# A two-layer decoder trunk: the second layer's modulation sums moved from VectorE to ScalarE and GpSimd, with three smaller moves beside them

## The chip, the cores and the metric

The kernel runs on one core of a Trainium2 chip. A core has five engines that work side by side: TensorE (PE in the profile; its weight loads are the row PEld), VectorE (DVE), ScalarE (ACT), GpSimd (POOL) and SyncE (SP), which here does nothing but issue transfers between the device's main memory and the on-chip memory. Each engine runs its own instructions in the order in which they were put there, and waits on semaphores for the others. The metric is device time in microseconds (us) of one launch. Results are compared by the median of several runs.

## The reference, cut to what matters

Everything is float32, for one sequence of 1024 positions of width 1024, in two layers:

```python
c_act = silu(c)                                    # one vector of 1024
for l in range(2):
    mod = c_act @ ada_w[l] + ada_b[l]              # 1024 x 6144: six vectors of 1024
    shift_m, scale_m, gate_m, shift_f, scale_f, gate_f = split(mod, 6)
    h = rms_norm(x, g_pre_mix[l]) * (1 + scale_m) + shift_m
    q, k, v, u = split(h @ w_in[l] + b_in[l])      # 512, 128, 128, 512
    attn = sliding-window attention with sinks and partial rotary (q, k, v)
    pool = causal means over 2, 4, 8, 16 positions of u, mapped and scaled
    x = x + gate_m * rms_norm(concat(attn, pool) @ w_out[l], g_post_mix[l])
    h = rms_norm(x, g_pre_ffn[l]) * (1 + scale_f) + shift_f
    f = (silu(h @ w_gate[l]) * (h @ w_up[l])) @ w_down[l]      # inner width 2816
    x = x + gate_f * rms_norm(f, g_post_ffn[l])
```

The vector `mod` depends on `c` and on the weights alone, so it can be made at any time before it is used. Its weights are 24 MB for each layer.

## The kernel before, in words

**Products.** A float32 operand is split into a rounded part `hi` (one ScalarE copy, line 213) and the rest `lo` (one VectorE subtraction, line 214; both stand in the helper `split`). A product is then three matmuls, hi by hi, hi by lo and lo by hi, into the same PSUM bank (`mm3`, lines 239, 242 and 243). One matmul has 128 x 128 weights and 512 columns. So each new operand costs ScalarE and VectorE one pass each, whatever TensorE does.

**Stages.** The 1024 positions are two halves of 512 (h = 0 and 1). In each layer come: the input projection (`q_pass`, `kv_pass`, `u_pass`) with attention and pooling beside it; the output projection (`mix_out`); the norm after it (`post_norm`); the upward product; the downward product (`down`); and the norm after that (`post_ffn`). A helper `run(stream, steps, (side, n))` writes one step of the main stream and then its share of the side streams' steps, so that side work is written between the main stream's steps. A scheduler then orders each engine's instructions, as far as their dependencies allow.

**The upward and downward products** use a scheme that replaces the eight products of 2 x 2 blocks by seven. The upward one goes over 11 pairs of 128-column blocks of gate and up weights (`up_pair`). Of a pair's seven products, two use only half 0 of the positions (`up_firsts`, tiles `hT`); they are made ahead for some pairs, and their results go to main memory and back (tile `firsts`). `FIRST = (3, 6)` says how many pairs are made ahead: three beside attention, six beside the norm of half 1. The other five products of a pair use sums of both halves (tiles `t1` to `t4` and `b22`), which `up_sums` makes after that norm. It is also the only place ahead of the downward product where GpSimd does arithmetic on tiles of 128 x 512 (lines 982 and 986). One product of a pair is 24 matmuls. Around it VectorE makes block sums of the weights (lines 1083, 1084, 1088 and 1089, tile `raw`), the `lo` parts, the sums of PSUM banks with earlier ones (line 1068, `<-acc`), and combinations of results (lines 1007 and 1102 to 1113).

**Modulation sums.** `c_act @ ada_w` for 512 columns is one job: eight rows of 128 x 512 are loaded in turns into the two buffers of tile `ar`, and VectorE multiplies each by a column of `c_act` and adds it to tile `ada` (lines 271 and 273). The result is split (`ph`), and two matmuls with the constant `picks` add it up over the partitions (lines 367 and 368 for shift and scale, 404 and 405 for a gate); `close` in `ada_pair` or `ada_gate` does the rest. The layer-1 jobs run in three places: the shift and scale of its first sub-layer beside layer 0's downward product (four jobs), and the first gate with the shift and scale of its second sub-layer beside layer 1's own projections (six jobs). Each layer's last gate (two jobs) runs beside its own upward product.

**Between the layers.** `post_ffn` of half 1 writes the normalised rows to main memory (tile `n`), and layer 1's `u_pass` reads them back block by block for the transposes (`transposed`, tile `raw`). Tiles live in three regions, `mix`, `up` and `down`, which reuse the same memory one after the other; tags such as `ph`, `hi`, `raw`, `ar`, `ada` and `G` are shared by all of them.

## Time and profile before

| | |
|---|---|
| runs (three) | 1945.44, 1948.76 and 1952.40 us; median 1948.76 us |
| the profiled execution | 1944.55 us, of which the span from its first to its last instruction is 1942.8 us |
| PE busy | 1874.0 us, 96% of the span |
| DVE busy | 1564.3 us, 81% |
| ACT busy | 954.5 us, 49% |
| POOL busy | 49.0 us, 3% |
| moved by DMA | 336.62 MB, mean 173 GB/s |

In the span, layer 0's projections and attention lie from about 20 to 280 us, its upward product from about 435 to 762 us and its downward product to about 990 us; layer 1's upward product runs to about 1720 us.

How to read it: a row of the windows gives, for each engine, busy time and the number of instructions in that stretch, then the clock that TensorE was granted (1.00 is full speed), the mean busy share of the 16 DMA engines, and GB/s. A row of the groups gives line, engine, operation, output and inputs, shape, count, busy us, mean ns of one, and idle time of the engine just before, with what ended it. A row of the waits reads "who waited for whom: us in total, times, longest".

### The profile page before, as it was taken

How to read it: one execution, taken by the hardware profiler on the slowest of the kernel's cores; microseconds unless marked ns; L12 is line 12 of the kernel's file. 1: busy time of each engine (PE TensorE's matmuls, PEld its weight loads, DVE VectorE, ACT ScalarE, POOL GpSimd, SP SyncE). 2: the span in 40 equal slices, each digit the busy share in tenths (PEclk: the TensorE clock that was granted, in tenths of full speed). 3: DMA queues.
4: the chain of work that ended last, by engine and by line, in shares of the span. 5: the costliest groups of instructions: out<-in, count | busy, mean ns of one | idle time of the engine just before them, and what ended most of it. 6: DMA issues, size and time to landing. Idle time of an engine off the chain costs nothing. (4 is left out here: it accounts for less than half of the span.)

```text
span 1942.8 us, 26040 instructions
## 1 busy us (share of the span) xinstructions
PE 1874.0 (96%) x8958; PEld 1541.0 (79%) x8958; DVE 1564.3 (81%) x2907; ACT 954.5 (49%) x1794; POOL 49.0 (3%) x100
## 2 busy tenths in 40 slices
PE   6999999999999999999999999999999999999997
PEld 4887778878888887778887878888778888878886
DVE  5999986779889886887878998756988888667687
ACT  4776785652222223445657668755522222235452
POOL 1000000020000000000000000000200000000000
PEclk9999999999999999999999999999999999999999
DMA  9345463556455446842556455535554644474343
GB/s 324 98 156 161 163 204 125 182 184 203 163 173 176 167 163 240 301 131 83 189 171 203 132 176 180 172 120 195 187 177 158 220 165 152 163 263 149 114 140 110
DMA packets 222052, 336.62 MB, mean 173 GB/s; under 512 B 16696, under 2 KB 120008, under 8 KB 221920
## 3 DMA queue, kind: packets, MB, share of 16 engines
q1 hardware_dynamic: 221776, 334.92, 52.2%
q8 instruction: 70, 1.15, 0.2%
q14 instruction: 62, 0.51, 0.1%
q0 software_dynamic: 32, 0.00, 0.0%
q10 hardware_dynamic: 112, 0.04, 0.0%
HBM read 262.00 MB, written 72.89 MB: 172 GB/s over the span
## 5 line engine op out<-in xcount | busy, mean ns | idle before, releaser
L213 ACT ACTIVATE hi<-raw 128x1024 fp32r<-128x1024 f32 (+1 forms) x388 | 332.5, 869 | 377.8 <-PE acc L242 220.7
L214 DVE TENSOR_TENSOR lo<-raw,hi 128x1024 fp32r<-128x1024 f32 (+1 forms) x388 | 382.9, 993 | 113.4 <-ACT hi L213 112.6
L239 PE MATMUL acc<-t,hi 128*128 128x512 f32 x704 | 276.7, 393 | 5.7 <-ACT hi L213 5.7
L243 PE MATMUL acc<-t,lo 128*128 128x512 f32 x704 | 276.1, 393 | 3.4 <-DVE lo L214 3.4
L242 PE MATMUL acc<-t,hi 128*128 128x512 f32 x704 | 276.0, 392 | 0.0
L243 PE MATMUL acc<-bh,lo 128*128 128x512 f32 x528 | 206.4, 391 | 0.0
L239 PE MATMUL acc<-bh,hi 128*128 128x512 f32 x528 | 203.5, 390 | 3.0 <-ACT bh L213 3.0
L239 PE MATMUL acc<-hT,hi 128*128 128x512 f32 x480 | 191.2, 398 | 7.8 <-ACT hi L213 7.2
L1068 DVE TENSOR_TENSOR fn<-acc,fn 128x512 f32<-128x512 f32 x220 | 151.1, 687 | 50.8 <-PE acc L243 50.2
L242 PE MATMUL acc<-hT,hi 128*128 128x512 f32 x480 | 188.3, 392 | 0.0
L243 PE MATMUL acc<-hT,lo 128*128 128x512 f32 x480 | 186.8, 393 | 0.9 <-DVE lo L214 0.9
L239 PEld LDWEIGHTS acc<-t,hi 128*128 128x128 f32 x704 | 133.5, 190 | 34.9 <-ACT hi L213 7.3
L243 PEld LDWEIGHTS acc<-t,lo 128*128 128x128 f32 x704 | 133.4, 190 | 34.2 <-DVE lo L214 6.5
L242 PEld LDWEIGHTS acc<-t,hi 128*128 128x128 f32 x704 | 133.5, 190 | 27.9
L242 PE MATMUL acc<-ph,hi 128*128 128x512 f32 x320 | 126.0, 394 | 1.3 <-DVE ph L214 1.1
L239 PEld LDWEIGHTS acc<-bh,hi 128*128 128x128 f32 x528 | 99.1, 188 | 24.6 <-ACT bh L213 3.8
L273 DVE SCALAR_TENSOR_TENSOR ada<-ar,c_act,ada 128x512 f32<-128x512 f32 x140 | 104.7, 748 | 17.0 <-DMA ar<-in_ada_w_dram 15.8
L243 PEld LDWEIGHTS acc<-bh,lo 128*128 128x128 f32 x528 | 99.6, 189 | 20.5
L239 PEld LDWEIGHTS acc<-hT,hi 128*128 128x128 f32 x480 | 90.7, 189 | 27.4 <-ACT hi L213 9.1
L1006 ACT ACTIVATE fn<-fn 128x512 f32<-128x512 f32 x44 | 27.9, 633 | 168.9 <-DVE fn L1068 168.9
L243 PEld LDWEIGHTS acc<-hT,lo 128*128 128x128 f32 x480 | 90.1, 188 | 19.5 <-DVE lo L214 1.3
L242 PEld LDWEIGHTS acc<-hT,hi 128*128 128x128 f32 x480 | 90.7, 189 | 17.3 <-issue 0.2
(302 smaller groups left out, 3866.6 us busy)
## 6 DMA issues: line engine op xcount, KB each, us to landing
ar<-in_ada_w_dram SPq DMA_DIRECT2D x160, 256.0 KB
raw<-in_w_gate_dram SPq DMA_DIRECT2D x44, 512.0 KB
raw<-in_w_up_dram SPq DMA_DIRECT2D x44, 512.0 KB
raw<-in_w_in_dram SPq DMA_DIRECT2D x80, 256.0 KB
raw<-keeps SPq DMA_DIRECT2D x40, 512.0 KB
keeps<-fn SPq DMA_DIRECT2D x66, 256.0 KB
two_b<-in_w_down_dram SPq DMA_DIRECT2D x30, 512.0 KB
raw<-keepa SPq DMA_DIRECT2D x25, 512.0 KB
```

Of the source, the lines that this page charges most:

```text
L213: nc.scalar.activation(hi, src, AF.Copy)
L214: nc.vector.tensor_sub(lo, src, hi.bitcast(F32))
L239: ins = nc.tensor.matmul(dst, lh, rh, start=first, stop=False)
L242: nc.tensor.matmul(dst, lh, rl, start=False, stop=False)
L243: return nc.tensor.matmul(dst, ll, rh, start=False, stop=last)
L273: nc.vector.scalar_tensor_tensor(acc, w, c_act[:, i : i + 1], acc, op0=ALU.mult, op1=ALU.add)
L1006: nc.scalar.activation(g, g, AF.Silu)
L1068: nc.vector.tensor_add(halves_of(dst)[m], bank, halves_of(src)[m])
```

## The change

There are five parts. The first is the largest.

1. **Layer 1's modulation sums under layer 0's upward product.** All ten jobs of layer 1's two shift-and-scale pairs and first gate move there, beside layer 0's last gate, so that twelve jobs stand there; layer 1's upward product keeps its own two. They use a new routine, `ada_beside`: ScalarE multiplies a row in place by its column of `c_act`, and GpSimd adds it to the sum; GpSimd also makes the `lo` part of the result. Rows are loaded three steps ahead into four buffers, the two of `ar` and the two halves of `G`. `close` runs three steps after the split. VectorE does none of these sums any more. Layer 0's first six jobs, beside its own projections, stay as they were.
2. **The closing matmuls keep their place**: both `picks` matmuls are ordered behind the most recent product written before them.
3. **`FIRST = (3, NPAIR - 3)`**: eight pairs instead of six are made ahead beside the norm of half 1, so all eleven are. The first operand of the first group is loaded and split while the pieces of half 0 are still being made.
4. **`down_prelude`**: the first operands of the downward product are made ahead of the `down` region, in tiles of shared tags.
5. **Between the layers** the `mix` region is opened ahead of `post_ffn` of half 1, which leaves its normalised rows in tile `cfb`; the four writes to main memory and the eight reads fall away.

```diff
+    recent = {}
     def split(hi, lo, src):
-        nc.scalar.activation(hi, src, AF.Copy)
+        recent["split"] = nc.scalar.activation(hi, src, AF.Copy)
         nc.vector.tensor_sub(lo, src, hi.bitcast(F32))
...
-        return nc.tensor.matmul(dst, ll, rh, start=False, stop=last)
+        recent["product"] = ins = nc.tensor.matmul(dst, ll, rh, start=False, stop=last)
+        return ins
...
-            nc.tensor.matmul(dst, pick, hi, start=r == 0, stop=False)
+            after(nc.tensor.matmul(dst, pick, hi, start=r == 0, stop=False), recent["product"])
...
+    def ada_beside(jobs):
+        AHEAD = 3
+        rows, sums, done = {}, {}, {}
+        for i in range(KD * len(jobs) + KD):
+            n, j = divmod(i - AHEAD, KD)
+            if j == 1 and n - 1 in sums:
+                acc = sums.pop(n - 1)
+                hi, lo = done[n - 1] = t_("ph", [P, 512], F32R), t_("ph", [P, 512], F32R)
+                after(nc.scalar.activation(hi, acc, AF.Copy), recent["split"])
+                nc.gpsimd.tensor_sub(lo, acc, hi.bitcast(F32))
+            if j == 4 and n - 1 in done:
+                jobs[n - 1][2](*done.pop(n - 1))
+            if i - AHEAD in rows:
+                w = rows[i - AHEAD]
+                after(nc.scalar.activation(w, w, AF.Copy, scale=c_act[:, j : j + 1]), recent["split"])
+                if j == 1:
+                    sums[n] = t_("ada", [P, 512])
+                    nc.gpsimd.tensor_add(sums[n], rows[i - AHEAD - 1], w)
+                elif j > 1:
+                    nc.gpsimd.tensor_add(sums[n], sums[n], w)
+            if i < KD * len(jobs):
+                l, n0, _ = jobs[i // KD]
+                if i % 4 == 0:
+                    G = t_("G", [P, D])
+                    rows[i], rows[i + 1] = halves_of(G)
+                elif i % 4 > 1:
+                    rows[i] = t_("ar", [P, 512])
+                nc.sync.dma_start(
+                    rows[i], ada_w[l].rearrange("(p j) n -> p j n", j=KD)[:, i % KD, n0 : n0 + 512]
+                )
+            yield
...
-    FIRST = (3, 6)
+    FIRST = (3, NPAIR - 3)
...
-        side = ada_jobs(l)
+        side = iter(()) if l else ada_jobs(0)
...
             for k in range(KD):
                 hts0.append(pre_norm_piece(k, par["abf"], None, fn, kept0[k]))
+                if k == KD - 3:
+                    next(firsts[0])
                 yield
...
-        nxt, jobs = None, []
+        nxt, jobs = None, ada_gate(l, 1)
         if l + 1 < DEPTH:
             nxt = layer_cols(l + 1)
-            jobs = ada_pair(l + 1, 0, nxt["cols"], nxt["abm"])
-        side = ada_stream(ada_gate(l, 1))
+            jobs += ada_pair(l + 1, 0, nxt["cols"], nxt["abm"]) + ada_gate(l + 1, 0)
+            jobs += ada_pair(l + 1, 1, nxt["cols"], nxt["abf"])
+        side = ada_beside(jobs)
...
-        run(ups(), 5 * NPAIR + 2 * (NPAIR - sum(FIRST)), (side, 2 * ADA + 4))
+        run(ups(), 5 * NPAIR + 2 * (NPAIR - sum(FIRST)), (side, (len(jobs) + 1) * KD))
         drain(side)
         G = load_gate(l, 1)
-        side = ada_stream(jobs)
-
+        prelude = down_prelude(wd, kept)
         region("down")
...
         if nxt:
-            drain(post_ffn(1, fn[1], ss[1], G, False))
+            region("mix")
+            xs1 = wide_tiles("cfb")
+            drain(post_ffn(1, fn[1], ss[1], G, xs1))
             par = nxt
```

Line numbers of the changed kernel differ: its `split` is lines 215 and 216, its `mm3` lines 241, 244 and 245, its PSUM sums line 1102.

GpSimd's instructions at the start of layer 0's upward product, before (`sa` and `ar` are the last sums of `up_sums`, `vz` the first of layer 1's attention):

```order
L982 TENSOR_TENSOR sa<-sa 128x512
L986 TENSOR_TENSOR ar<-ar,sa 128x512
L715 CAST vz<-vz_zero 128x64 x2
L723 CAST vz<-vz_zero 128x64 x3
L715 CAST vz<-vz_zero 128x64 x2
```

and in the change, one job's rows of the twelve (`ada` is the sum, `G` and `ar` hold the scaled rows):

```order
L1020 TENSOR_TENSOR ar<-ar,sa 128x512
L453 TENSOR_TENSOR ada<-G 128x512
L455 TENSOR_TENSOR ada<-ada,ar 128x512 x2
L455 TENSOR_TENSOR ada<-ada,G 128x512 x2
L455 TENSOR_TENSOR ada<-ada,ar 128x512 x2
L445 TENSOR_TENSOR ph<-ada,ph 128x512
```

Between the last sum of `up_sums` and layer 1's attention GpSimd had nothing; now it has twelve times these eight instructions.

ScalarE in the middle of layer 0's upward product, before (`hi<-raw` splits a product's weights, `fn` and `sb` are the gates' silu):

```order
L213 ACTIVATE hi<-raw 128x1024 x4
L1006 ACTIVATE sb<-sb 128x512
L1006 ACTIVATE fn<-fn 128x512
L213 ACTIVATE hi<-raw 128x1024
L1006 ACTIVATE fn<-fn 128x512
```

and in the change:

```order
L215 ACTIVATE hi<-raw 128x1024
L450 ACTIVATE G<-G,c_act 128x512
L450 ACTIVATE ar<-ar,c_act 128x512
L1040 ACTIVATE fn<-fn 128x512
L215 ACTIVATE hi<-raw 128x1024
L450 ACTIVATE ar<-ar,c_act 128x512
L450 ACTIVATE G<-G,c_act 128x512
L215 ACTIVATE hi<-raw 128x1024
L444 ACTIVATE ph<-ada 128x512
```

One or two scalings of a row now stand between two splits of weights.

SyncE in the same place of the change (rows into `G` and `ar`, weights of the next pair into `raw`; before, the four `raw` loads followed each other with at most a row or two of `ar` between them):

```order
L463 DMA G<-in_ada_w_dram 128x512 x2
L463 DMA ar<-in_ada_w_dram 128x512 x2
L1087 DMA raw<-in_w_gate_dram 128x4x256
L463 DMA G<-in_ada_w_dram 128x512 x2
L463 DMA ar<-in_ada_w_dram 128x512
L1087 DMA raw<-in_w_up_dram 128x4x256
```

Row loads, each of which waits for its buffer's last reader on GpSimd, now stand ahead of weight loads in the one queue.

More of the change, by code (lines that the diff above doesn't have):

```diff
@@ L403, in close @@
             bank = msc_bank()
-            nc.tensor.matmul(bank[0:1, :], picks[:, 3:4], hi, start=True, stop=False)
+            after(nc.tensor.matmul(bank[0:1, :], picks[:, 3:4], hi, start=True, stop=False), recent["product"])
             nc.tensor.matmul(bank[0:1, :], picks[:, 3:4], lo, start=False, stop=True)
@@ L476, in pre_norm_raw, with transposed @@
         return hf
[L478 to L486 removed]
+    def transposed(k, prev, xs):
+        src = [xt[:, k * P : (k + 1) * P] for xt in xs]
         bank = msc_bank()
@@ L1322, in hybrid_decoder_kernel @@
         if l:
-            region("mix")
             layer_rows(l, par)
```

119 lines of the change are left out of this document (59 added, 60 removed).

## The prediction, on record before the changed kernel was run

> **What bounds the kernel now.** I read the page first, then the busy time by stretches, then who ended TensorE's waits in the stretches that the change touches.
>
> ```profile
> span 1942.8 us, 26040 instructions
> PE 1874.0 (96%) x8958; PEld 1541.0 (79%) x8958; DVE 1564.3 (81%) x2907; ACT 954.5 (49%) x1794; POOL 49.0 (3%) x100
> ```
>
> TensorE is busy for 1874.0 of 1942.8 us, so all that a change can win without taking matmuls away is 68.8 us, of which the start and the end hold some 20. This change takes no matmul away. It can only close gaps, or open some. The stretches (the second is a part of the first):
>
> ```profile
> core 0: us, PE busy (x) PEld busy (x) DVE busy (x) ACT busy (x) POOL busy (x), PEclk, DMA share, GB/s
> 446.00:762.00 316.00, 315.73 (x1391) 260.46 (x1391) 264.60 (x339) 84.98 (x100) 0.00 (x0) 1.00 0.52 175
> 450.00:500.00 50.00, 50.00 (x222) 41.36 (x221) 46.22 (x60) 13.92 (x17) 0.00 (x0) 1.00 0.56 193
> ```
>
> Layer 0's upward product has no gap to close: TensorE 315.73 of 316 us. VectorE is next, 264.60 us (84%), and in the fullest 50 us it was at 46.22 (92%) without costing TensorE anything. GpSimd is empty. So this is the stage with nothing to win and the least room, and the new work goes there. The gaps are elsewhere, at the borders of stages:
>
> ```profile
> PE acc L239 <- ACT bh L213: 1.5, 1, 1.5
> PE msc L367 <- ACT ph L213: 2.1, 2, 1.4
> PE msc L368 <- DVE ph L214: 2.0, 2, 1.3
> PE acc L242 <- DVE ph L214: 1.1, 3, 0.7
> PE msc L367 <- ACT ph L213: 0.7, 2, 0.5
> PE msc L368 <- DVE ph L214: 0.3, 1, 0.3
> PE msc L489 <- DMA raw<-n: 1.3, 1, 1.3
> PE acc L239 <- ACT hi L213: 2.0, 1, 2.0
> PE acc L239 <- ACT hi L213: 1.8, 1, 1.8
> PE acc L243 <- DVE lo L214: 1.5, 2, 1.1
> PE acc L239 <- ACT hi L213: 3.9, 2, 3.1
> PE acc L243 <- DVE lo L214: 0.9, 2, 0.7
> ```
>
> These are TensorE's waits in seven windows, in this order. One row of 760 to 766 us, from the upward to the downward product (the same row stands at 1716 to 1724 in layer 1). Three of 790 to 845, the closing matmuls of four modulation jobs in the downward product. Two of 1129 to 1151, those of layer 1's jobs beside its projections. One of 1026 to 1028, the rows read back between the layers. One of 270 to 278, the first product made ahead (again at 1229 to 1235 in layer 1). Two of 430 to 448, the norm of half 1 before the upward product. Two of 1387 to 1430.5, the same in layer 1. Some gaps cost twice, since the granted clock is low behind them:
>
> ```profile
> 270.00:280.00 10.00, 8.00 (x44) 6.65 (x43) 7.08 (x18) 9.19 (x22) 0.23 (x1) 0.83 0.73 233
> 435.50:442.30 6.80, 5.73 (x14) 4.48 (x15) 6.66 (x9) 1.80 (x3) 2.13 (x1) 0.50 0.39 128
> 822.00:846.00 24.00, 20.45 (x81) 15.65 (x80) 21.96 (x30) 11.40 (x21) 0.00 (x0) 0.93 0.55 176
> 1384.00:1402.00 18.00, 14.00 (x47) 10.19 (x47) 17.70 (x21) 10.21 (x15) 3.73 (x2) 0.81 0.51 164
> ```
>
> **What GpSimd costs VectorE.** The price of the move is not on GpSimd itself. `up_sums` already runs its eight additions of the same shape; these are VectorE's groups in that stretch, 404.9 to 438.3 us, then a row of the group of `hi`/`lo` splits from 490 to 630 us, where GpSimd is idle, then GpSimd's own:
>
> ```profile
> L214 DVE TENSOR_TENSOR t<-sa,t 128x512 fp32r<-128x512 f32 x8 | 7.5, 952 | 0.2
> L214 DVE TENSOR_TENSOR t<-ar,t 128x512 fp32r<-128x512 f32 x7 | 4.8, 681 | 0.2 <-ACT t L213 0.2
> L214 DVE TENSOR_TENSOR lo<-raw,hi 128x1024 fp32r<-128x1024 f32 x3 | 4.7, 1578 | 0.0
> L214 DVE TENSOR_TENSOR b<-sa,b 128x512 fp32r<-128x512 f32 x4 | 4.2, 1050 | 0.6 <-ACT b L213 0.6
> ...
> L1036 DVE TENSOR_TENSOR sb<-acc,sa 128x512 f32<-128x512 f32 x4 | 2.7, 678 | 0.0
> L1084 DVE TENSOR_TENSOR raw<-raw 128x1024 f32<-128x1024 f32 x1 | 2.3, 2320 | 0.0
> ...
> L214 DVE TENSOR_TENSOR lo<-raw,hi 128x1024 fp32r<-128x1024 f32 x26 | 31.6, 1222 | 0.6 <-ACT hi L213 0.5
> ...
> L986 POOL TENSOR_TENSOR ar<-ar,sa x8: 1290/1297/2131, 408.7 to 1391.9; 128x512 f32<-128x512 f32 x8
> ```
>
> A VectorE instruction with two inputs on chip is 681 ns where it is not met, and 952 or 1050 in the groups that GpSimd's additions meet; 1222 ns becomes 1578 and 2320. The one with an input from PSUM (`acc`) keeps 678. The excess is 8 x 0.271 + 4 x 0.369 + 3 x 0.356 + 1.10 = 5.8 us for eight GpSimd instructions: **0.73 us of VectorE for each**. GpSimd is held up too: 1297 ns at best, 2131 at worst.
>
> The Trainium skill ("SBUF — State Buffer", Who interferes with whom) has it as an exclusive lock: a VectorE instruction with two SBUF inputs and a GpSimd one that reads SBUF hold the shared pair for the whole instruction. The trace agrees on who is hit (678 against 1050). By the rule every such meeting would cost up to the whole 1.30 us, and with two thirds of VectorE's time here in such instructions the stage's term below would be some 13 us larger.
>
> **The change part by part.** *Layer 0's upward product, after.* It keeps 11 x 5 products of 24 matmuls, 222 to 50 us: 297 us of TensorE. The four products of the last two pairs move ahead, at equal cost. VectorE's work there, by the rows of 446 to 762 us:
>
> ```profile
> 446.00:762.00 316.00, 17.30 (x24) 1.25 (x2) 1.00 0.52 175
> ...
> L1068 DVE TENSOR_TENSOR sa<-acc,fn 128x512 f32<-128x512 f32 x4 | 2.8, 688 | 2.7 <-PE acc L243 2.7
> L1007 DVE TENSOR_TENSOR sa<-sa 128x512 f32<-128x512 f32 x2 | 1.4, 693 | 0.2
> ...
> L407 DVE TENSOR_TENSOR ar<-ar 1x512 f32<-1x512 f32 x2 | 1.3, 672 | 0.0
> L406 DVE TENSOR_TENSOR ar<-msc,ar 1x512 f32<-1x512 f32 x2 | 1.3, 670 | 0.0
> ```
>
> The first row is the same stretch for tile `ada` alone: 17.3 us of VectorE go. The two moved pairs take 2.8 + 1.4 + 4 x 1.22 = 9.1 us along; the second gate's closing brings 2.6. So 264.6 - 17.3 - 9.1 + 2.6 = 241 us are left. GpSimd gets 12 jobs x 8 = 96 instructions; at 0.73 us VectorE is held for 70 us more: **311 us, against 297 of TensorE**. VectorE becomes the bound. If it ran without any pause the stage would take 311 us (+14), at the best share seen, 92%, 337 us (+39). I take the middle, **+26 us**. The bounds: nothing, if every GpSimd instruction fell beside a PSUM addition or a pause (241 us fit in 297); and 96 x 1.30 = 125 us, if each held VectorE for its whole length: 366 / 0.924 = 396, +99. I stay near 0.73, since two thirds of VectorE's rows there are of the kind that was hit.
>
> ScalarE gets 96 scalings and 12 splits of about 0.63 us, the price of the same shape in its split `ph` (1.25 us for 2, above): 68 us on 85, well within 297. The rows add 96 - 24 loads of 0.26 MB, 19 MB, to a stretch at 175 GB/s and 0.52 of the DMA engines: about 0.72. Both are hidden, unless the order binds (rival 2). GpSimd itself needs 96 x 1.3 to 2.1 = 125 to 200 us: hidden. In layer 1, 16 such instructions (12 us of VectorE) stand for the 17 us taken away: nothing.
>
> *The downward product of layer 0* loses its closings: 2.1 + 2.0 + 1.1 = 5.2 us of waits, and the low clock, 24 x 0.07 = 1.7. VectorE has no sums there that would be late next. I count 6.9 in full. *The prelude* makes the first operands ahead: 1.5 in each layer, 3.0, in full. Its tiles are free of the region, so nothing but the last product is ahead of them.
>
> *Layer 1's projections* lose the closings' 0.7 + 0.3 and the read-back's 1.3: 2.3. *The first operand made earlier*: 2.0 in each layer and 10 x 0.17 = 1.7 of clock: 5.7. *Two more pairs beside the norm* give four products, 96 matmuls, 21.6 us of cover: 1.8 + 1.5 in layer 0, 3.9 + 0.9 in layer 1, and behind each the low clock (14 matmuls where full speed does 30 in 6.8 us, part of it the wait itself: 2.5 each): 13.1. These three make 21.1. They hang on chains in which another wait can come next (attention's VectorE steps beside the projections, the last `up_sums` before the upward product), so I take half, 10.5. Without their cover they return in full. The 16 small weight loads and the reloads of `firsts` that the two pairs add are no more than the four writes and eight reads that go.
>
> One loss more: the last closings now stand on TensorE in front of the first downward product, behind GpSimd's chain: 1 us.
>
> Sum, against the profiled execution: 1944.6 + 26 + 1 - 6.9 - 3.0 - 10.5 = **1951 us**. That execution lies 4.2 us under the median of the three runs, so for a median I forecast **1955 us**.
>
> The Trainium skill ("TensorE: Matmul & The Clock Gate", Part 1) lets the clock drop after an idle window of about 3.4 us. The rows above show 0.50 behind gaps of 1.8 and 1.1 us, so the measurement decides; by the page's rule the low clock behind these gaps would not be theirs to win, and the sum would be some 5 us higher.
>
> **The rivals.** *1. GpSimd is absorbed, and the kernel gets faster.* VectorE at 92% cost TensorE nothing, so up to 0.924 x 297 = 274.6 us of VectorE the stage stays at 297. That is (274.6 - 241) / 96 = 0.35 us for each GpSimd instruction. A third of VectorE's time is PSUM additions, and 16% of the stage was idle; if the meetings fall there half as often as in `up_sums`, this holds. Against it: the 0.73 was measured with PSUM additions in between. Then only gains are left: 1955 - 26 - 1 = 1928 us. Chance 0.27.
>
> *2. The order binds.* Weight loads stand behind row loads on SP's queue, and a row load waits for a GpSimd instruction; ScalarE's splits stand behind scalings that wait for rows. If the pair's weights come late by one held GpSimd instruction (2.1 us) and its scaling (0.6), 11 pairs lose 30 us more: about 1985 us. For it: the two buffers of weights leave little time. Against it: rows are loaded three steps ahead, and 104 steps lie over 297 us, so some 8 us. Chance 0.15.
>
> *3. The gaps stay.* The moves at the borders do nothing, since the next wait takes their place, and only the downward product's 6.9 us are won: 1955 + 13.5 = about 1968 us. Chance 0.08.
>
> **How the numbers follow.** My forecast has 0.50, with 1943 to 1968 us as its own range. The range over all leaves out a part of rivals 1 and 2: **1925 to 1988 us**. A measurement of this kernel can tell about 0.3% from no change, 5.8 us: slower is above 1954.6 us, faster below 1942.9. Slower: half of the forecast's and all of rivals 2 and 3, 0.25 + 0.23 = 0.48, and some more since the forecast's upper half is the wider: 0.50. Faster: rival 1 and a little of the forecast, 0.28. No change: 0.22.
>
> **What would show it.** In the changed profile, layer 0's upward product takes longer than 297 us, VectorE is above 92% in it, and its groups `lo<-raw,hi` and `raw<-raw` have means well over 1222 ns, with `fn<-acc,fn` still at 687; TensorE's waits there are `<-DVE lo`. If the stage is 297 us, rival 1 is right and the price of 0.73 wrong. If TensorE waits there for ScalarE behind DMA of `ar` or `G`, or VectorE waits for `raw`, it is rival 2. The downward product of layer 0 should have no wait on `picks`, the two borders no gap of 1.5 us, and the windows before the two upward products a clock near 1.00; where these rows stand unchanged, rival 3 holds.

## The result, and the profile after

| | |
|---|---|
| before, run beside it | 1948.17 us, median of 4 runs |
| after | 1998.47 us, median of 4 runs (1998.15 to 2001.52) |
| ratio | 1.0266, 95% interval 1.0251 to 1.0281: slower |
| forecast | 1955 us, range 1925 to 1988 |

The direction was the forecast's; the size was not, and the range did not hold it. The page of the changed kernel begins:

```profile
span 1996.9 us, 26224 instructions
PE 1893.3 (95%) x8958; PEld 1550.5 (78%) x8958; DVE 1529.4 (77%) x2781; ACT 1019.7 (51%) x1906; POOL 252.4 (13%) x212
```

VectorE was busy 35 us less than before, and TensorE 19 us more with the same number of matmuls: it ran some of them at a lower clock. The 54.1 us between the spans of the two profiled executions are divided here by stage, cut at the first and last matmul of each upward product (`acc<-t` and `acc<-b`). The four products that the change moves ahead of each upward product are 96 matmuls, 21.6 us; they are taken off the stage before the change and added to the one ahead of it:

| stage | before | after | difference |
|---|---|---|---|
| up to layer 0's upward product | 434.7 + 21.6 = 456.3 | 456.5 | +0.2 |
| layer 0's upward product | 327.4 - 21.6 = 305.8 | 386.6 | **+80.8** |
| layer 0's downward product | 226.8 | 215.1 | -11.7 |
| to layer 1's upward product | 402.3 + 21.6 = 423.9 | 410.0 | -13.9 |
| layer 1's upward product | 329.1 - 21.6 = 307.5 | 307.5 | 0.0 |
| to the end | 222.5 | 221.2 | -1.3 |

So one stage lost everything. Its window in the two kernels, before (with the four products) and after; the columns are those of the prediction's windows:

```profile
434.70:762.10 327.40, 325.89 (x1420) 267.61 (x1420) 275.72 (x353) 89.64 (x105) 2.13 (x1) 0.99 0.52 175
```

```profile
456.50:843.10 386.60, 335.18 (x1347) 263.36 (x1348) 284.06 (x320) 146.03 (x202) 170.29 (x96) 0.92 0.60 195
```

VectorE, which was to be the bound, is busy for 284.06 of 386.60 us: 73%. No engine is full. TensorE stands for 51 us, and the clock granted to it falls to 0.92 of full speed. The waits of that window, of SP's queue (SPq) too, first before and then after:

```profile
SPq L1071 <- DVE sb L1102: 60.7, 11, 7.8
SPq L1053 <- DVE lo L214: 54.9, 20, 6.2
```

```profile
SPq L463 <- POOL ada L455: 118.6, 38, 11.4
SPq L463 <- POOL ada L453: 41.5, 12, 6.9
SPq L1087 <- DVE lo L216: 0.8, 1, 0.8
PE acc L245 <- DVE lo L216: 30.2, 14, 4.1
PE acc L241 <- ACT hi L215: 21.7, 10, 5.8
ACT hi L215 <- DVE raw L1118: 58.3, 10, 9.0
DVE raw L1117 <- DMA raw<-in_w_up_dram: 25.6, 6, 5.9
DVE raw L1117 <- DMA keepa<-sb: 17.0, 3, 7.1
ACT G L450 <- DMA G<-in_ada_w_dram: 35.6, 13, 3.7
ACT ar L450 <- DMA ar<-in_ada_w_dram: 8.4, 6, 3.2
```

Line 1053 before is line 1087 after: the loads of the gate and up weights. The reader should look at this pair first. Before, those loads stood 54.9 us in the queue *for a free buffer*, that is, the queue was ahead of the engines and every load began at the first possible moment. After, they never wait for a buffer (0.8 us): when the queue reaches them the buffer has long been free. The queue is late, because it stands 160 us for GpSimd, to have a place for the next row (line 463). One pair shows it; SP's queue, then VectorE's, then TensorE's idle times:

```profile
606.70 2.56 SPq L463 DMA_DIRECT2D ar<-in_ada_w_dram  x2
609.36 0.39 SPq L1087 DMA_DIRECT2D raw<-in_w_gate_dram  x1
612.35 0.80 SPq L463 DMA_DIRECT2D G<-in_ada_w_dram  x2
614.80 0.33 SPq L463 DMA_DIRECT2D ar<-in_ada_w_dram  x1
615.18 0.43 SPq L1087 DMA_DIRECT2D raw<-in_w_up_dram  x1
616.16 0.33 SPq L463 DMA_DIRECT2D ar<-in_ada_w_dram  x1
616.59 0.39 SPq L1087 DMA_DIRECT2D raw<-in_w_gate_dram  x1
617.02 0.50 SPq L1087 DMA_DIRECT2D raw<-in_w_up_dram  x1
617.57 0.50 SPq L1091 DMA_DIRECT2D fn<-firsts  x1
```

```profile
617.98 0.68 DVE L1102 TENSOR_TENSOR fn<-acc,fn 128x512 f32<-128x512 f32 x1
624.13 1.23 DVE L1117 TENSOR_TENSOR raw<-raw 128x1024 f32<-128x1024 f32 x1 [5.48 <-DMA fn<-firsts]
```

```profile
627.81 0.51 PE L241 MATMUL acc<-t,hi 128*128 128x512 f32 x1 [2.39 <-ACT hi L215]
631.21 0.79 PE L245 MATMUL acc<-t,lo 128*128 128x512 f32 x1 [2.66 <-DVE lo L216]
```

The first weight load is issued at 609.36, the second behind three row loads at 615.18, the last at 617.02. VectorE then stands for 5.48 us before it can add up the new weights; the profile puts the end of this wait down to `fn<-firsts`, the load issued behind them. TensorE stands twice in its turn. Behind that the clock drops:

```profile
630.00:635.00 5.00, 3.79 (x9) 3.02 (x10) 5.00 (x6) 0.63 (x1) 2.20 (x2) 0.51 0.67 193
```

The groups of VectorE and GpSimd in the stage look only in part as the prediction said they would:

```profile
L216 DVE TENSOR_TENSOR lo<-raw,hi 128x1024 fp32r<-128x1024 f32 (+1 forms) x57 | 90.4, 1588 | 29.8 <-ACT hi L215 29.6
L1102 DVE TENSOR_TENSOR fn<-acc,fn 128x512 f32<-128x512 f32 x109 | 73.9, 681 | 13.8 <-PE acc L245 13.5
L1117 DVE TENSOR_TENSOR raw<-raw 128x1024 f32<-128x1024 f32 x10 | 12.3, 1226 | 48.1 <-DMA raw<-in_w_up_dram 25.6 <-DMA keepa<-sb 17.0 <-DMA fn<-firsts 5.5
L455 POOL TENSOR_TENSOR ada<-ada,ar 128x512 f32<-128x512 f32 x48 | 88.4, 1841 | 131.7 <-ACT ar L450 129.0
```

The splits went from 1222 to 1588 ns; the sums with an input in PSUM took 681 ns, 687 before. The block sums of weights, `raw<-raw`, hardly changed: their four groups have means of 1213 to 1299 ns. Counted over the trace, 51 of the 56 splits of that size overlap an instruction of GpSimd, and only 3 of the 42 block sums do. Line 1117, the first block sum of a pair, shows how late the weights are: VectorE idles 48.1 us ahead of it, 1.0 us before the change. GpSimd itself idles before most of its additions: it is not short of time.

### The profile page after: what moved, and what is told of

Same layout as the page of the kernel before. It is cut to its first block, busy times and chain, and to the rows that moved or that the text cites. A ratio compares the mean times of both kernels' runs of the same rounds, so it can differ in the third digit from the quotient of the medians.

```text
span 1996.9 us, 26224 instructions
## 1 busy us (share of the span) xinstructions
PE 1893.3 (95%) x8958; PEld 1550.5 (78%) x8958; DVE 1529.4 (77%) x2781; ACT 1019.7 (51%) x1906; POOL 252.4 (13%) x212
## 4 chain that ended last, share of the span: by engine, by line
PE 43%; DVE 8%; DMA 3%; ACT 2%; issue 1%; POOL 0%; SPq 0%; DVEq 0%; ACTq 0%; POOLq 0%
PE acc L245 13%; PE acc L241 13%; PE acc L244 13%; DVE lo L216 2%; DMA raw<-in_w_up_dram 1%; DVE fn L1102 1%; PE msc L848 1%; DMA raw<-in_w_gate_dram 1%; DMA ar<-x 1%; DVE fn L569 0%; ACT hi L215 0%; ACT sb L832 0%; PE msc L518 0%; PE pv L241 0%; DVE fn L570 0%
## 5 line engine op out<-in xcount | busy, mean ns | idle before, releaser
L216 DVE TENSOR_TENSOR lo<-raw,hi 128x1024 fp32r<-128x1024 f32 (+1 forms) x388 | 407.7, 1055 | 160.3 <-ACT hi L215 159.9
L245 PE MATMUL acc<-t,lo 128*128 128x512 f32 x704 | 285.7, 406 | 33.4 <-DVE lo L216 33.0
L241 PE MATMUL acc<-t,hi 128*128 128x512 f32 x704 | 285.1, 405 | 23.2 <-ACT hi L215 23.1
L244 PE MATMUL acc<-t,hi 128*128 128x512 f32 x704 | 283.0, 402 | 0.0
L245 PE MATMUL acc<-bh,lo 128*128 128x512 f32 x520 | 202.3, 389 | 0.0
L245 PEld LDWEIGHTS acc<-t,lo 128*128 128x128 f32 x704 | 137.7, 196 | 72.7 <-DVE lo L216 43.8
L241 PEld LDWEIGHTS acc<-t,hi 128*128 128x128 f32 x704 | 137.9, 196 | 57.7 <-ACT hi L215 28.8
L1102 DVE TENSOR_TENSOR fn<-acc,fn 128x512 f32<-128x512 f32 x220 | 149.1, 680 | 26.0 <-PE acc L245 25.6
L244 PEld LDWEIGHTS acc<-t,hi 128*128 128x128 f32 x704 | 137.9, 196 | 29.5
L455 POOL TENSOR_TENSOR ada<-ada,ar 128x512 f32<-128x512 f32 x56 | 104.6, 1868 | 221.0 <-ACT ar L450 218.3
L241 PEld LDWEIGHTS acc<-bh,hi 128*128 128x128 f32 x520 | 97.6, 188 | 20.4
L245 PEld LDWEIGHTS acc<-bh,lo 128*128 128x128 f32 x520 | 97.6, 188 | 20.4
L241 PEld LDWEIGHTS acc<-hT,hi 128*128 128x128 f32 x480 | 90.3, 188 | 26.3 <-ACT hi L215 8.3
```

The costliest lines, as they stand in the source:

```text
L216: nc.vector.tensor_sub(lo, src, hi.bitcast(F32))
L241: ins = nc.tensor.matmul(dst, lh, rh, start=first, stop=False)
L244: nc.tensor.matmul(dst, lh, rl, start=False, stop=False)
L245: recent["product"] = ins = nc.tensor.matmul(dst, ll, rh, start=False, stop=last)
L455: nc.gpsimd.tensor_add(sums[n], sums[n], w)
L1102: nc.vector.tensor_add(halves_of(dst)[m], bank, halves_of(src)[m])
```

## The experiments

Two theories stood at the start. **L**: GpSimd's additions slow VectorE, as the prediction priced it, only more. **Q**: the row loads in SP's queue wait for GpSimd and make the weight loads behind them late. All ratios are to the kernel before, run beside on the same chip; a difference between two experiments is worked out from their ratios times 1949 us. "The stage" is layer 0's upward product.

### Part 1 alone is the loss

```diff
 e2: the changed kernel with part 1 undone (parts 2 to 5 stay)
-        side = iter(()) if l else ada_jobs(0)
+        side = ada_jobs(l)
...
-        side = ada_beside(jobs)
+        side = ada_stream(ada_gate(l, 1))
```

> The change without its first part: the modulation sums stay where they were before, on VectorE; the order of the closing matmuls, eleven pairs made ahead, the prelude and the rows kept on chip stay in. Both theories: layer 0's upward product is back at 297 to 310 us. If the 28 us that the changed kernel wins between layer 0's downward and layer 1's upward product come from the other parts, about 1915 us; if they come from VectorE being relieved there, about 1943 us.

1935.8 us, ratio 0.9933 (0.9915 to 0.9951). Parts 2 to 5 win 13 us, between the two figures expected for them; part 1 loses 65. Its window of the stage, and those of the two stages behind it, downward product and layer 1's projections:

```profile
456.40:762.80 306.40, 302.20 (x1325) 247.86 (x1326) 262.04 (x338) 81.74 (x95) 0.00 (x0) 1.00 0.55 188
762.80:985.50 222.70, 217.77 (x968) 176.28 (x967) 175.98 (x250) 118.38 (x191) 2.31 (x7) 1.00 0.55 186
985.50:1406.00 420.50, 408.04 (x2170) 340.83 (x2168) 341.45 (x811) 278.02 (x611) 21.11 (x36) 1.00 0.53 166
```

```profile
843.10:1058.20 215.10, 214.76 (x962) 176.63 (x961) 159.11 (x223) 115.90 (x187) 2.31 (x7) 1.00 0.48 166
1058.20:1468.20 410.00, 402.15 (x2154) 339.51 (x2153) 306.38 (x748) 272.86 (x604) 19.69 (x36) 1.00 0.44 142
```

The second fence is the changed kernel. Moving the sums takes 7.6 and 10.5 us off these two stages. TensorE's idle time falls from 4.9 + 12.5 to 0.3 + 7.9 us: 9.2 us. Its busy time falls by 3.0 + 5.9 = 8.9 us. Of these, 22 matmuls (the closings), an estimated 5 us at the 0.227 us from one to the next, only moved into the upward product. So part 1 had 9 us of idle time to win, 13 if the rest of the busy time is counted too.

### Rows, additions, and the queue

```diff
 e1: rows loaded by GpSimd
-                nc.sync.dma_start(
+                nc.gpsimd.dma_start(
 e3: two rows loaded once for each layer, all scalings and additions made on them
+                if i == 0:
+                    halves = halves_of(t_("G", [P, D]))
+                rows[i] = halves[i % 2]
+                if i < 2:
                     nc.sync.dma_start(
 e4: the changed kernel with narrow additions
-                    nc.gpsimd.tensor_add(sums[n], sums[n], w)
+                    nc.gpsimd.tensor_add(sums[n][:, 0:64], sums[n][:, 0:64], w[:, 0:64])
```

> The changed kernel with its row loads issued from GpSimd's own queue instead of SyncE's; additions, scalings and bytes are the same. Theory Q (the queue): in SyncE's queue a row load waits for a GpSimd addition and the weight loads behind it come late; VectorE waits 48 us for weights in layer 0's upward product. Then these waits go, the stage falls from 390 us to 311 to 335, and the time to 1920 to 1945 us. Theory L (the lock): GpSimd's additions hold VectorE, and the late weights only follow from that; the stage stays at 370 to 390 us and the time at 1978 to 2000 us.

1980.5 us, 1.0162 (1.0140 to 1.0185), and a stage of 371.6 us: both at the lower edge of Theory L's ranges. 20 us of the loss are back.

> The changed kernel, but only the first two rows of a stage's modulation jobs are loaded and then scaled and added again and again, so the sums are made of the wrong rows; 92 + 14 row loads and their waits are left out, every scaling and every addition stays. Theory Q: as in the run with rows from GpSimd's queue or a little lower, the stage 311 to 335 us, 1915 to 1942 us; if only that run is fast and this one too, bytes do not matter, and if only this one is fast, it is the bytes. Theory L: 1975 to 2000 us.

1939.6 us, 0.9958 (0.9940 to 0.9976), in Theory Q's range. With every scaling and every addition in place and only two rows loaded, 60 us of the loss are gone.

> The changed kernel, but six of a job's seven additions on GpSimd are made over 64 of 512 columns, so the sums are incomplete; rows, waits, scalings and order stay. GpSimd then holds VectorE for well under half as long. Theory L: the excess of VectorE goes, the stage falls to 300 to 315 us, and the time to 1912 to 1930 us. Theory Q: a row's buffer comes free only some 1.5 us earlier, behind a scaling that stays where it is; the time stays at 1960 to 1995 us.

1966.5 us, 1.0091 (1.0068 to 1.0113): 34 us from short additions, again in Theory Q's range. One run speaks for one theory and two for the other, and short additions and missing rows each give a large part back: neither theory is enough alone. So the next four divide the loss: the additions without rows (e7), the row loads with no engine waiting for them (e6), the waits with an eighth of the bytes (e8), and a row's lead (e5).

```diff
 e7: e3 with the narrow additions of e4
 e6: e3, and every other row loaded again into the ar places, read by nobody
+                nc.sync.dma_start(rows[i] if i < 2 else t_("ar", [P, 512]), ...)
 e8: the changed kernel with 64 of 512 columns of each row loaded
-                    rows[i], ...[:, i % KD, n0 : n0 + 512]
+                    rows[i][:, 0:64], ...[:, i % KD, n0 : n0 + 64]
-                after(nc.scalar.activation(w, w, AF.Copy, scale=c_act[:, j : j + 1]), ...)
+                after(nc.scalar.activation(w, <a constant tile>, AF.Copy, scale=c_act[:, j : j + 1]), ...)
 e5:
-        AHEAD = 3
+        AHEAD = 2
```

> e3 with six of seven additions of each sum made on 64 of the 512 columns, as in e4. The modulation sums are left wrong. It measures the term that the prediction summed (GpSimd's additions lengthen VectorE's instructions) without the rows. In e3 the first layer's upward product took 333.2 us, against 306.4 in e2, of which some 8.6 us are 22 more products of TensorE in that stage (the closings of ten sums). Theory L (the rest is VectorE slowed by GpSimd): the stage falls to 318 us or less and the time to 1925 us or less. If it is ScalarE's 96 scalings that hold up the splits, the time stays at 1936 to 1941 us.

1918.7 us, 0.9845 (0.9827 to 0.9864); the stage is 316.0 us. Both figures of Theory L came: the full additions cost 22 us (e7 to e3). Their price in VectorE's time can be read from the two windows, e3 and then e7:

```profile
453.10:786.30 333.20, 314.59 (x1347) 251.59 (x1348) 288.82 (x320) 148.12 (x202) 174.22 (x96) 0.98 0.45 154
```

```profile
455.00:771.00 316.00, 309.53 (x1347) 250.68 (x1348) 262.51 (x321) 146.02 (x202) 92.47 (x96) 0.99 0.48 162
```

VectorE is 26.3 us shorter with 72 additions narrowed: 0.37 us for each. That is the difference between a full and a narrow one. For the whole price an estimate starts from e2, where GpSimd does nothing in the stage: 262.0 us of VectorE, less 17.3 for the sums that it makes itself there, and some 4.5 more for the closings of ten more jobs, are 249 us. Against that e3 is 40 us longer, 0.41 us for each of 96 instructions, and the changed kernel (284.06) 35 us, 0.36. The prediction had 0.73.

> e3 (scalings and additions all made, on two rows that are loaded once for each layer) with every other row loaded again in SP's queue, into the two ar places, where no engine reads it. The modulation sums are wrong, as in e3; bytes and their queue are those of the changed kernel, but no load waits for an addition and no scaling waits for a load. Theory W: as e3, 1938 to 1945 us. Theory S: as e3 too, 1938 to 1945 us. Theory B: as the changed kernel, 1985 to 2000 us.

1960.6 us, 1.0055 (1.0040 to 1.0070). None of the three theories had this number. The row loads cost 19 us although no engine waits for them (e3 to e6); what the changed kernel has on top of e6, 41 us, comes from the rows being waited for. But the 19 us are not the bytes alone. The unread rows take turns in two places, and SP's queue stands for its own earlier loads:

```profile
SPq L461 <- DMA ar<-in_ada_w_dram: 62.2, 51, 5.1
SPq L1086 <- DVE lo L216: 45.6, 16, 5.9
```

The weight loads (line 1086) wait 45.6 us for their buffer, 71.7 in e3: a part of the queue's lead is lost here too. Whether the 19 us are slower transfers or this standing, the run does not tell.

> The changed kernel with the first 64 of the 512 columns of each row loaded (32 KB for 256 KB), and each scaling writing the whole row from a constant tile, after its load; the sums are wrong. The number of loads, their place in the queue, and what each waits for and is waited for are as in the changed kernel; seven eighths of the bytes are gone. Theory W: 1980 to 1998 us. Theory B: 1938 to 1950 us. Theory S: the rows land sooner after their issue, but their issue is as late, so part of it: 1960 to 1985 us.

1978.4 us, 1.0145 (1.0125 to 1.0166), in Theory S's range and just under Theory W's. The same from the other side: an eighth of the bytes, and 24 us come back. The waits stay in kind but shrink, SP's for GpSimd from 160 to 98.2 + 30.4 = 129 us, so the 24 us are not the bytes alone either. With e6 this says that row loads cost something when nobody waits for them, and more when they are waited for.

> The changed kernel with one constant changed: a row is scaled two steps of its generator after its load is issued, not three. All loads, scalings and additions stay. With three steps and four places for rows, the load that takes both halves of G can only start when the addition of the same step has been made; with two it waits for the addition of the step before. Theory W (the 59 us that e3 took off are waits of SP's queue for a place, with the weight loads behind them): the waits of SP for GpSimd in the first layer's upward product fall from 160 us to under 60 and the time to 1965 us or less. Theory B (it is the 24 MB more that are moved in that stage, which slow the weight loads): nothing changes, 1990 to 2000 us. Theory S (it is ScalarE standing at a scaling whose row has not landed, with the splits of weights behind it): a row has one step less to land, so ScalarE waits longer for rows and the time is 2005 us or more.

1990.7 us, 1.0211 (1.0194 to 1.0228). A step less between load and use gives 11 us, and SP still waits 95.0 + 43.0 = 138 us for GpSimd. Theory B had this number, but e6 and e8 leave it a part only. By the waits, the step that was to set SP free was no use, since GpSimd's addition still waits for ScalarE's scaling (158 us, 166 in the changed kernel), ScalarE has splits of weights ahead of it, and these wait for weights. Four places for rows tie the queue to that circle; this is read from the waits and was not tested by itself.

### Which wait: ScalarE's for a row, or the weight loads' in the queue

```diff
 e9: ScalarE scales a constant into a tile that nobody reads; GpSimd adds the rows unscaled
+                apart = t_("junk", [P, 512], BF16).rearrange("p (o n) -> p o n", o=4)
-                after(nc.scalar.activation(w, w, AF.Copy, scale=c_act[:, j : j + 1]), ...)
+                after(nc.scalar.activation(apart, <a constant tile>, AF.Copy, scale=c_act[:, j : j + 1]), ...)
 e10: e9 with the rows loaded by GpSimd
```

> The changed kernel with each scaling on ScalarE reading a constant tile and writing a tile that nobody reads, and GpSimd adding the rows as they were loaded; the sums are wrong, since no row is multiplied by c. All row loads (in SP's queue, each waiting for the addition that frees its place), all 96 scalings and all additions stay, but ScalarE waits for no row. From e7 to the changed kernel there are now three steps of 21, 21 and 38 us: full additions, the rows' bytes, and the waits that rows bring. This run and the next divide the last. Theory Q (SP's queue stands for GpSimd, and the weight loads behind it are late): 1990 to 2000 us, and SP still waits over 100 us for GpSimd. Theory S (ScalarE stands at scalings whose rows have not landed): 1958 to 1966 us. Theory QS (half each, as e1's 18 us suggest): 1975 to 1985 us.

2000.8 us, 1.0276 (1.0243 to 1.0309), as the changed kernel. ScalarE waits for no row any more, the 35.6 + 8.4 = 44 us of the changed kernel are gone, and nothing is won. SP's wait for a row's place fell from 160 to 97 us, a little below the 100 that Theory Q named, and that won nothing either. What remains in the queue and at VectorE:

```profile
SPq L465 <- POOL ada L457: 55.9, 30, 4.8
SPq L465 <- POOL ada L455: 41.3, 11, 6.0
DVE raw L1119 <- DMA raw<-in_w_up_dram: 24.5, 4, 7.6
```

> The same with the row loads issued by GpSimd, as in e1: no load of weights is behind a row load, and ScalarE waits for no row. The sums are wrong in the same way. Theory QS: what is left are the additions and the bytes, as in e6: 1957 to 1966 us. Theory S: the same. Theory Q: as e1, 1978 to 1983 us, since e1 had already freed the queue; then what keeps e1 above e6 by 20 us is the issue of loads by GpSimd itself, which e6 has not.

1982.9 us, 1.0178 (1.0152 to 1.0204), as e1 and as Theory Q said. ScalarE's standing for rows is out. Theory Q is left. It was then tested by itself: the order of the queue was changed, and nothing else.

```diff
 e14: the weight loads of the next pair written inside the pair before
         bank = times(a21, T1)
+        if p + 1 < NPAIR:
+            weights(p + 1, 0)
...
         bank = times(a22, T4)
+        if p + 1 < NPAIR:
+            weights(p + 1, 1)
```

> The changed kernel, complete, with the weight loads of the next pair of columns issued inside the pair before, as soon as their buffer has been used (the first two after the fifth of its seven products, the other two after the last), ahead of the row loads of the steps in between. Rows, scalings, additions, bytes and buffers are the same. Theory Q (weight loads stand behind row loads in SP's queue; e6 against e9 puts it at 38 us): a part comes back, as far as the queue's order is changed, 1965 to 1988 us, and VectorE's wait for weights falls below 15 us from 25.6. If weights are late because of the bytes or because GpSimd's additions make everything late, it stays at 1993 to 2003 us.

1973.6 us, 1.0112 (1.0091 to 1.0133): 30 us come back, with the same work, bytes and buffers. Its waits in the stage:

```profile
SPq L463 <- POOL ada L455: 102.6, 30, 10.4
SPq L1089 <- DVE lo L216: 15.4, 10, 3.5
DVE raw L1125 <- DMA raw<-in_w_up_dram: 17.7, 6, 4.2
PE acc L245 <- DVE lo L216: 21.4, 17, 3.5
PE acc L241 <- ACT hi L215: 13.4, 11, 3.9
```

The queue stands for GpSimd nearly as long as before, but with fewer weight loads behind it: they wait for their buffer again (15.4 us, line 1089), and TensorE's two waits fall from 51.9 to 34.8 us. VectorE's wait for weights fell less than forecast, to 17.7 and not under 15. ScalarE now waits longer for rows (52.5 us for `G`, 35.6 in the changed kernel), and the kernel is faster all the same. So the order of the queue is a cause. How much of the 30 us belongs to the 41 is open: a load issued earlier also has more time to land, and that can take back some of the 19 us of e6.

### What is left in GpSimd's queue

In e1 the weight loads waited 63.2 us for their buffer again, so SP's queue was ahead as before, and still only 20 us came back; e1 stayed 21 us above e6. Three runs looked for the rest.

```diff
 e12: e3, and in each step a load of 16 columns issued by GpSimd into a small tile
 e13: e12 with each of them tied behind the addition of its step
+                    after(load, last[-1])
 e15: e13 with whole rows, into the ar places, read by nobody
```

> e3 (two rows loaded once for each layer, all scalings and additions made; the sums are wrong) with one load of 16 columns (8 KB in 128 pieces) issued by GpSimd in each step, into small tiles that nobody reads: the number of loads of e1, nearly without their bytes. In e1 and e10 GpSimd issued 89 to 91 loads at 0.55 us in the first layer's upward product, 50 us of its time, VectorE was busy 297 us there against 284.5 in e6, and both kernels ended 20 us above e6. Theory G (issuing loads is itself work of GpSimd that slows VectorE, so e1 gave back what it had freed in SP's queue, and the queue's waits are the whole 38 us of the last step): 1955 to 1965 us, and VectorE busy 8 us or more longer than the 288.8 of e3. Theory N (it costs nothing, and e1 shows the queue's share, 18 of 38): 1937 to 1944 us.

1946.1 us, 0.9989 (0.9970 to 1.0009), and it says nothing on the question: the scheduler issued the loads from 111 us on, ahead of the stage, since nothing held them.

> e12 with each of GpSimd's small loads tied behind the addition of its step, since in e12 nothing held them and they were all issued between 111 and 260 us, before the stage in question: e12 told nothing on it. Otherwise the same (scalings and additions on two rows loaded once; the sums are wrong). Theory G (issuing loads is work of GpSimd that costs VectorE, and e1 and e10 gave back 20 us by it): 1953 to 1965 us, with VectorE busy 8 us or more longer in the first layer's upward product than the 288.8 of e3. Theory N (issuing costs nothing): 1936 to 1944 us, VectorE within 3 us of e3; then what holds e1 and e10 20 us above e6 is that the rows are read, and GpSimd waits for them.

1942.8 us, 0.9966 (0.9948 to 0.9985). 92 loads, each 551 ns of GpSimd, in the stage, and VectorE's busy time is 288.57 us against 288.82 in e3. The issuing costs VectorE nothing here, as Theory N said.

> e13 with whole rows (512 columns, 256 KB) in GpSimd's loads, into the two ar places, read by nobody; the sums are wrong as in e3. It is e6 with GpSimd instead of SP as the issuer of the row loads. e6 was 1960.6 us, e10 (rows by GpSimd, added by GpSimd) 1982.9. Theory D (bytes that go through GpSimd's queue disturb the weight loads or VectorE more than the same bytes in SP's queue): 1975 to 1985 us. Theory R (the bytes cost the same, and what is left in e1 and e10 comes from the rows being read, so that additions are late when a row is late): 1957 to 1966 us.

1982.9 us, 1.0174 (1.0146 to 1.0203): the number of e10, and in Theory D's range. The same row loads that cost 19 us in SP's queue cost 40 in GpSimd's. But why is not settled. In this run GpSimd stood for its own earlier loads (and 19.8 us more for the `ar` tiles of the closings), and ScalarE's scalings, made in place, stood behind GpSimd longer than in e13 (there 24.6 and 24.4 us):

```profile
POOL ar L466 <- DMA ar<-in_ada_w_dram: 49.0, 27, 5.7
ACT G L450 <- POOL ada L455: 37.1, 27, 4.5
ACT G L450 <- POOL ada L453: 35.2, 9, 8.0
```

So it may be that bytes moved through GpSimd's queue cost the others more, or that GpSimd's standing does. The runs do not part the two.

### Half of it

```diff
 e11: six sums beside the upward product, the other six where they were
-        side = iter(()) if l else ada_jobs(0)
+        side = ada_jobs(l)
...
-            jobs += ada_pair(l + 1, 0, nxt["cols"], nxt["abm"]) + ada_gate(l + 1, 0)
-            jobs += ada_pair(l + 1, 1, nxt["cols"], nxt["abf"])
+            jobs += ada_pair(l + 1, 0, nxt["cols"], nxt["abm"])
```

> The changed kernel with six of its twelve sums (the first layer's second gate and the second layer's first pair) made beside the first layer's upward product, and the other six where they were before, on VectorE under the second layer's projections; nothing is left out. Six sums over the same stretch: a row every 6 us instead of every 3. In e2, where VectorE makes all sums, TensorE idles 4.9 us in the first layer's downward product and 11.4 in the second layer's projections; after the change 0.3 and 6.8. So the whole gain of moving the sums is some 9 us, and of this version some 4. Theory P (the loss goes with the number of rows): half of the 63 us between e2 and the changed kernel, less what is left of the gain: 1960 to 1970 us. Theory T (a threshold: the loss comes when rows are wanted faster than four places, a load and a contended addition can give them, and when VectorE, at 262 us of 306 in e2, is filled): 1930 to 1940 us, about e2.

1957.3 us, 1.0040 (1.0021 to 1.0059), a little under Theory P's range and 21 us above e2: a third of the loss for half of the sums. The stage took 330.0 us, 23.6 more than in e2, and the downward product and projections together 5.8 less. So the move is not free at half the rate either; a lower rate was not run. The fastest complete version is e2, without part 1.

## Why the prediction was wrong, step by step

**The step that failed** is the sum's first term, "I take the middle, +26 us", with the last closings' +1: it measured +80.8. Its own mechanism was there, and came out near that size: e3, in which the additions and scalings run as forecast and only two rows are loaded, has a stage of 333.2 us, +27.4. But two things that the prediction had put aside came on top: the row loads themselves (19 us) and the waits for rows, with the weight loads behind them in the queue (41 us).

*The bytes*: "the rows add 19 MB ... about 0.72. Both are hidden". The DMA share in e6 is 0.66, near that figure, and the unread rows cost 19 us. So a mean share of 0.66 over a stage did not mean that there was room. That weights are wanted in bursts, and that rows fill the same moments, is a reading of the traces and was not tested; a part may be the queue's 62.2 us of standing for its own rows.

*The queue*: this was rival 2, described rightly (weight loads behind row loads, which wait for GpSimd), and used wrongly. It was weighed as an alternative to the term, with 0.15, when it comes in addition to it: the waits for rows made 41 us, against the +30 that rival 2 gave, and writing the weight loads earlier brought 30 back (e14). "Rows are loaded three steps ahead ... some 8 us" spoke against it; e5, with a step less, was 11 us faster, so more lead was no protection. Rival 2's other half, ScalarE's splits behind scalings that wait for rows, is real in the rows (44 us of waits), but taking those waits away won nothing (e9).

**The price of 0.73 us** was too high: 0.36 us in the changed kernel and 0.41 in e3, by the estimate above. The 241 us to which it was added were too low: they were counted from 446 us on, and the stage begins at 434.7; by e2 they are some 249. "VectorE becomes the bound" was wrong: at 73% in the changed kernel and 87% in e3 it was never full. That the term came out near its size in e3 is therefore partly luck: the price was too high, the base too low, and the stage holds the 22 moved closings, some 5 us, which the term put at nothing. The rule of the Trainium skill that stood beside it ("SBUF — State Buffer", Who interferes with whom: the shared pair is an exclusive lock, for which a VectorE instruction with two SBUF inputs contends with a GpSimd one that reads SBUF) is no better as a price: full holding would be 1.30 us for each addition, against 0.36 to 0.41. Which instructions are hit is as that section of the Trainium skill says: `fn<-acc,fn` took 681 ns, and `lo<-raw,hi` 1588.

**The clock** behind gaps was counted at the borders (1.7 to 2.5 us each) and not in this stage. The stage is 80.2 us longer than in e2: 47.2 of it are TensorE's standing (51.4 us against 4.2), and 33.0 are longer busy time. Of these the closings make some 5 and the lower clock, granted at 0.92 in the mean, an estimated 28.

**The gains** were forecast at 20.4 us. The stages other than the upward product won 11.7 + 13.9 + 1.3 - 0.2 = 26.7; without the estimated 5 us of matmuls that only moved, 21.7. So the sum of the gains was nearly right. Point by point:

- *The downward product and the prelude*, 6.9 + 1.5, measured 11.7, of which an estimated 1.4 are 6 moved matmuls: right in kind and a little low. TensorE's busy time there is 214.76 of 215.10 us.
- *Layer 1's projections, the first operand, two more pairs*: taken at half, 10.5 over both layers. Layer 1 won 13.9, of which an estimated 3.6 are 16 moved matmuls. In layer 0 nothing came in sum (+0.2), though its border closed in part: the two waits of 1.75 and 1.12 us at the first product are 0.7 and 0.6 in the changed kernel. (The 1.3 us of the read-back, given for 1026 to 1028 us, are those of a wider window, 1024 to 1044.)
- *The second prelude*, 1.5, measured 1.3.

**Rival 1** (absorbed) needed 0.35 us for each addition. The 0.36 to 0.41 of the estimate are close to it, and still e3 lost 22 us to the additions, with VectorE at 87%: that it is late in the moments that count, though it has time on average, is argued from this and not shown by itself. **Rival 3** (the gaps stay) is out: parts 2 to 5 won 13 us in e2, and even at layer 0's border the gaps shrank. Why the sum won nothing there is open.

**The signs named beforehand**: the stage above 297 us, the mean of `lo<-raw,hi` and `fn<-acc,fn` came as said. "VectorE above 92%" did not, and `raw<-raw`, named beside `lo<-raw,hi`, stayed at 1213 to 1299 ns. TensorE's waits were for VectorE's `lo` (30.2 us) and for ScalarE's `hi` too (21.7). Rival 2's sign, VectorE waiting for `raw` behind DMA, was there with 25.6 us, and by the prediction's own rule decided for it.

## What to carry to other kernels

Before adding transfers to a queue, look at what its critical loads wait for: if they wait for their own buffer, the queue is ahead, and it stays ahead only as long as nothing in front of them waits for a slower engine; count that as a cost in addition to the work's own, and write the critical loads first. A queue that is ahead is not enough: in e1 and e15 the weight loads waited over 60 us for their buffer again, and both kernels still lost. Ask what a move has to win (here 9 us of TensorE's idle time) before adding up what it may cost. And here a stage whose bound engine is full, with a second one at 84%, was the wrong place for new work, even though the engines that took it were idle.

## What the runs showed that was not expected

- Gaps of 2.39 and 2.66 us in the trace above are followed by 5 us at a granted clock of 0.51. Matmuls at full speed come back some 6 us after the second gap, so standing costs more than its own time. The section that the prediction cited (the Trainium skill, "TensorE: Matmul & The Clock Gate", Part 1: an idle window of about 3.4 us) would leave each of these gaps without a penalty. Together they are 5.05 us with two matmuls between, and no run here tells whether by that rule they would count as one window.
- Row loads of 256 KB that no engine reads or waits for cost 19 us in SP's queue (e6) at a DMA share of 0.66, and 40 us when GpSimd issues them (e15), both with the reservations above: the issuing queue stood for its own earlier loads. Issuing itself, 551 ns of GpSimd for each load, cost VectorE nothing (e13).
- An addition on GpSimd cut from 512 to 64 columns still took 694 ns in the mean in e7, against 1795 in e3. The shortest ones took 318 and 1285 ns, so more than half of the narrow one's mean is not its own work; that it stands for VectorE is the likely reading.
